# A hybrid layer on one core: a table of steps for the inputs of the output projection, and token sums in pieces of two steps

## The chip, the cores and the metric

The kernel runs on one core of a Trainium2 chip. The metric is the device time of one execution in microseconds. The kernel before took 2541.38 us in the median of three runs (2538.63 to 2546.69). The profiled execution is another run, 2547.02 us long.

## The reference

One layer over 2176 tokens of width 1024: 128 context tokens and 2048 latent ones, in float32. For each token:

```python
h = rmsnorm(x, norm1) * (1 + scale1) + shift1
z = h @ w_in                                   # conv parts b, c, x; q, k, v, o, gates
y_sc = sc_b * conv3(sc_c * sc_x)               # short gated convolution, 512 wide
h_m  = rmsnorm(mlstm_bidir(q, k, v, gates)) * mh_norm * sigmoid(o)   # 4 heads of 128
x = x + gate1 * (concat([y_sc, h_m]) @ w_out)  # the output projection
h2 = rmsnorm(x, norm2) * (1 + scale2) + shift2
a, g = split(conv3(h2 @ w_up))                 # 2 x 2816 wide, conv over the grid
x = x + gate2 * ((silu(g) * a) @ w_down)
```

It returns the normalised x of both token groups and the final scan states of the context.

## The kernel before

Float32 products are made of three TensorE products each: every operand is split into a high part (a copy that rounds, on ScalarE) and a low part (the difference, on VectorE or GpSimd), and high*high, low*high and high*low are added up in PSUM (lines 221 to 223). A product of one 128-wide weight block with one block of up to 384 tokens is a *step* of 24 such matmuls. Tokens lie in six blocks: five of 384 and one of 256. The results of successive steps go to two PSUM buffers by turn (`acc`), so the product of step n+2 waits for the eviction of step n.

Names of tiles: `wst` is a weight as loaded (two buffers), `wh` and `wl` its split (four buffers); `xt` half a block of y as loaded (two buffers), `hH` and `hL` its split; `row` rows of results or of x; `F` a tile of 128x2304 with two buffers; `tH`, `tL` the split token sums. Tiles whose names end in D lie in DRAM. All DMAs are issued from one queue on SyncE (SP), which works in order: a DMA that must wait holds up those behind it.

The phases: modulation; v, gates, k, q and o products with scans of the gates; then three stretches that matter here.

1. **Sums weave.** Units of the backward chunk scan run beside the steps of the q and o heads. The o heads (`oD`) come last.
2. **Mix weave.** 34 units (17 chunks, two pairs of heads) of the mLSTM itself run beside 1.6 steps each. The steps are first the 36 of the short convolution (four output rows, three blocks, three products), then the output projection's 48: three groups of two token blocks, sixteen steps in a group (four pairs of output rows; in each pair two steps of the one block and two of the other). Each group needs y, which convolution and units have written to DRAM, loaded and split (L506, L517, L518). The evictions of the output projection are L604, its squares L566 and their sum L572; `stats` (five steps behind a group's end) makes the factors rc that the normalisation needs. In a unit, `queries` and `weigh` make R (L972, L976), which the y products (L986, L988) use; `denom` begins with the update of the forward state sf (L995), then come the denominators and in `heads` the division.
3. **Sums and up-projection.** The up-projection multiplies by sums of token blocks, seven forms ("slots" 0 to 6, used in the order 6, 0, 1, 5, 2, 4, 3), in the manner of Strassen. `sums` makes them in pieces beside the last steps of the output projection: a piece loads two stretches of x, scales them (L272, L274), forms four sums (L276 to L279), splits some of them straight into a slot (L283, L284: "direct") and stores the others (L287). A slot that isn't split directly is loaded again by `get_f` (L302) and split by `put_f` (L312, L313). The products of the up-projection are L1206 to L1208, from 1106.41 us on; the down-projection follows.

Until the Mix weave a scheduler orders the instructions; from the first Mix instruction on (`first`) every engine runs them in the order in which the program emits them (`in_order`).

Of the kernel before, what the change touches and what calls it, by code (L numbers as in the profile page):

```python
# [10 lines left out]
F32 = mybir.dt.float32  # L11
# [7 lines left out]
P = 128  # L19
# [38 lines left out]
def hymba_kernel(ctx: ExitStack, tc: tile.TileContext, I, O):  # L58
# [182 lines left out]
    def sums(hf, pool, qs=range(2), direct=()):  # L241

        for q in qs:
# [18 lines left out]
            nf = load(0)  # L262
            yield
            for kk in range(4):
                f = nf
                if kk < 3:
                    nf = load(kk + 1)
                for i, k in ((4, kk + 4), (6, kk)):
                    x = f[:, i * w:(i + 2) * w]
                    for i0, n, v in ((0, P, 0), (P, 2 * w - P, 1)) if ts[0] == 0 else ((0, 2 * w, 1),):  # L270
                        e = i0 + n
                        V.scalar_tensor_tensor(x[:, i0:e], x[:, i0:e], ab[:, 1, k, v:v + 1], rb[:, i0:e],  # L272
                                               op0=ALU.mult, op1=ALU.mult)
                        S.activation(x[:, i0:e], x[:, i0:e], AF.Identity, bias=modT[:, 24 + k, v:v + 1])  # L274
# [13 lines left out]
                if kk < 3:  # L288
                    yield
# [62 lines left out]
    with ExitStack() as ph1:  # L352
# [24 lines left out]
        def vg(blocks, hs, ws):  # L377
            for b in blocks:
                hH, hL = hs[b]
                for j in range(2):  # L380
                    for c in chunks(b):
# [8 lines left out]
                        r = rq.tile([P, 2, 129], F32, name="rv", bufs=4)  # L390
# [30 lines left out]
        def shortconv(blocks, hs, then=None, more=(), ws=None):  # L421
# [3 lines left out]
            ws = [] if ws is None else ws  # L425
            ws += [load_w(next(todo)) for _ in range(3)]
# [15 lines left out]
            for m in range(4):  # L442
                wc, wx, wb = ws[:3]
                del ws[:3]
                for j, b in enumerate(blocks):
                    t0, n = BL[b]
                    store()
                    if then and m == 3 and j:
                        then(j - 1, 0)
# [3 lines left out]
                    if j < 2:  # L453
                        get()
                    else:
                        split()
                    yield
                    acc = gemm(wx, hs[b], n)
# [13 lines left out]
                    if then and m == 3 and j:  # L472
                        then(j - 1, 1)
                    yield
                    acc = gemm(wb, hs[b], n)
# [6 lines left out]
                    if then and m == 3 and j:  # L482
                        then(j - 1, 2)
# [15 lines left out]
        def get_y(b):  # L499

            assert done >= set(chunks(b))
            t0, n = BL[b]
            yts = []
            for kh in range(2):
                yt = xp.tile([P, 4, 384], F32, name="xt")
                Q.dma_start(yt[:, :, :n], yD[4 * kh:4 * kh + 4, :, t0:t0 + n].rearrange("k p t -> p k t"))  # L506
                yts.append(yt)
            return yts

        def split_y(b, yts, kh):  # L510

            n = BL[b][1]
            if kh == 0:
                early[b] = h_pair()
            yH, yL = early[b]
            for k in range(4):
                S.activation(yH[:, 4 * kh + k, :n], yts[kh][:, k, :n], AF.Copy)  # L517
                V.tensor_sub(yL[:, 4 * kh + k, :n], yts[kh][:, k, :n], yH[:, 4 * kh + k, :n].bitcast(F32))  # L518

        held_y = {}  # L520

        def load_y(b, step):
            if step == 0:
                held_y[b] = get_y(b)
                if b:
                    next(outs)
            else:
                split_y(b, held_y[b], step - 1)

        def next_y(grp, ready):  # L530


            for b, may in zip(grp, ready):
                while not done >= set(chunks(b)):
                    yield
                yts = get_y(b)
                yield
                for kh in range(2):
                    while not may():
                        yield  # L540
                    split_y(b, yts, kh)
                    yield

        def out_proj(grps, defer, ws):


# [27 lines left out]
            rows, got, behind, squared, held, sss, past = [], [], [], [], [], {}, set()  # L574
            for k in range(2):
                load_r(k)
            ny = iter(())
            yield
            for k, (g, m, b) in enumerate(steps):
                grp, (t0, n) = grps[g], BL[b]  # L580
                if k % 16 == 0 and g + 1 < len(grps):
                    ny = next_y(grps[g + 1], (lambda: True, lambda b=grp[0]: (b, KT - 1) in past))
# [11 lines left out]
                if k % 16 >= 5:  # L594
                    next(ny, None)
# [10 lines left out]
                past.add((b, m))  # L606
                behind.append((b, m, xr))
                if k % 16 == 15:
                    run(ny)
                    held = [k, grp]  # L610
                if k == len(steps) - 1:
                    for x in squared + [close(*x) for x in behind]:
                        add(*x)
                    defer.append(lambda: stats(grp, [sss[b] for b in grp]))
                yield
# [315 lines left out]
        class Mix:  # L931
# [58 lines left out]
            def denom(self):  # L990
                c, hp, sf = self.c, self.hp, sfs[self.hp]
                if 0 <= c < NL - 1:
                    for h in range(2):
                        r = c * 4 + 2 * hp + h
                        V.scalar_tensor_tensor(sf[:, h], sf[:, h], decB[:, r:r + 1], self.sb[:, h, 0],  # L995
# [473 lines left out]
```

## Time and profile before

| | us |
|---|---|
| median of 3 runs (lowest to highest) | 2541.38 (2538.63 to 2546.69) |
| profiled execution | 2547.02 |
| its span, first to last instruction | 2545.2 |
| TensorE busy (share) | 2464.8 (97%) |
| VectorE busy (share) | 1664.6 (65%) |
| ScalarE busy (share) | 1122.8 (44%) |
| GpSimd busy (share) | 573.7 (23%) |
| mean granted TensorE clock | 0.987 |
| last head product done, first shortconv product | 621.5, 629.75 |
| first product of the up-projection | 1106.41 |

Engines are PE (TensorE), DVE (VectorE), ACT (ScalarE), POOL (GpSimd) and SP (SyncE, which issues the DMAs). A row of a timeline gives start and duration, the line of the kernel, the operation with its tiles, a count, and in brackets the idle time before it with what ended it. In the table of windows each engine's busy time and count is followed by the granted clock of TensorE, the DMA engines' busy share and GB/s.

### The profile page before, as it was taken

The numbers are of one execution on the slowest core, as the hardware profiler recorded it, in microseconds if no ns is written. First come the engines' busy times: TensorE is split into PE (matmuls) and PEld (weight loads), VectorE is DVE, ScalarE is ACT, GpSimd is POOL, SyncE is SP. The second block draws the span as 40 slices with busy tenths as digits, with TensorE's granted clock in tenths as the row PEclk, the third lists the DMA queues.
The fourth block names the chain that finished last, engine by engine and source line by source line (L and its number), as shares of the span: only waits on it lengthen the run. The fifth ranks groups of instructions, "written<-read, shape, count | busy, mean of one in ns | idle before, by whom it ended". The sixth has DMA issues, their size and how long they took to land.

```text
span 2545.2 us, 42525 instructions
## 1 busy us (share of the span) xinstructions
PE 2464.8 (97%) x16127; PEld 2360.4 (93%) x16127; DVE 1664.6 (65%) x2670; ACT 1122.8 (44%) x2059; POOL 573.7 (23%) x501
## 2 busy tenths in 40 slices
PE   7999999998999999889999999899999999999998
PEld 7999999998999989889999999788888899999998
DVE  3993552331556676688677666877767786787586
ACT  4421162333444554455444444555545554444342
POOL 2442242110343443322122111221221100000000
PEclk9999999999999999999999999999999999999999
DMA  8873873455666876755224122522222276867674
GB/s 282 279 241 116 305 242 96 126 177 166 209 208 204 285 243 221 250 199 174 83 99 165 73 74 83 183 98 84 92 98 84 80 248 207 251 195 225 188 222 133
DMA packets 281424, 444.60 MB, mean 175 GB/s; under 512 B 23283, under 2 KB 206723, under 8 KB 279555
## 3 DMA queue, kind: packets, MB, share of 16 engines
q1 hardware_dynamic: 281218, 441.88, 52.9%
q8 instruction: 127, 2.08, 0.3%
q14 instruction: 79, 0.64, 0.1%
HBM read 335.31 MB, written 106.48 MB: 174 GB/s over the span
## 4 chain that ended last, share of the span: by engine, by line
PE 68%; DVE 5%; DMA 4%; issue 2%; ACT 1%; POOL 0%; SPq 0%; DVEq 0%; ACTq 0%; POOLq 0%
PE pa L1206 7%; PE pa L1208 6%; PE pa L1207 6%; PE d L1361 5%; PE d L1362 5%; PE d L1360 5%; PE acc L221 4%; PE acc L223 4%; PE acc L222 4%; PE pb L1206 3%; PE pb L1207 3%; PE pb L1208 3%; PE pc L1206 2%; PE pc L1207 2%; PE pc L1208 2%
## 5 line engine op out<-in xcount | busy, mean ns | idle before, releaser
L221 PE MATMUL acc<-hH,wh 128*128 128x384 f32 (+1 forms) x1536 | 514.6, 335 | 23.3 <-DVE row L604 14.6
L223 PE MATMUL acc<-hH,wl 128*128 128x384 f32 (+1 forms) x1536 | 507.8, 331 | 0.4 <-POOL wl L130 0.4
L222 PE MATMUL acc<-hL,wh 128*128 128x384 f32 (+1 forms) x1536 | 506.7, 330 | 0.0
L1206 PE MATMUL pa<-tH,wh 128*128 128x288 f32 (+1 forms) x1056 | 348.7, 330 | 12.1 <-issue 7.3
L1360 PE MATMUL d<-bh,wh 128*128 128x272 f32 x1232 | 356.7, 290 | 0.7 <-ACT raw L1218 0.7
L1362 PE MATMUL d<-bh,wl 128*128 128x272 f32 x1232 | 357.1, 290 | 0.0
L1361 PE MATMUL d<-bl,wh 128*128 128x272 f32 x1232 | 356.3, 289 | 0.0
L1208 PE MATMUL pa<-tH,wl 128*128 128x288 f32 (+1 forms) x1056 | 347.9, 329 | 1.0 <-DVE wl L331 1.0
L1207 PE MATMUL pa<-tL,wh 128*128 128x288 f32 (+1 forms) x1056 | 347.6, 329 | 0.0
L331 POOL TENSOR_TENSOR wl<-st,wh 128x512 fp32r<-128x512 f32 x132 | 185.3, 1403 | 704.3 <-ACT wh L330 677.8
L130 POOL TENSOR_TENSOR wl<-wst,wh 128x512 fp32r<-128x512 f32 (+1 forms) x160 | 236.5, 1501 | 419.2 <-ACT wh L127 373.1
L221 PEld LDWEIGHTS acc<-hH,wh 128*128 128x128 f32 x1536 | 292.6, 190 | 26.2 <-issue 15.4
L222 PEld LDWEIGHTS acc<-hL,wh 128*128 128x128 f32 x1536 | 292.8, 191 | 0.3 <-issue 0.2
L223 PEld LDWEIGHTS acc<-hH,wl 128*128 128x128 f32 x1536 | 292.0, 190 | 1.1 <-POOL wl L130 0.9
L1149 DVE SCALAR_TENSOR_TENSOR tt<-raw,fw,tt 128x127 f32<-128x127 f32 (+4 forms) x264 | 246.4, 955 | 2.7 <-ACT tt L1155 1.4
L1360 PEld LDWEIGHTS d<-bh,wh 128*128 128x128 f32 x1232 | 232.9, 189 | 1.3 <-ACT raw L1218 1.1
L1361 PEld LDWEIGHTS d<-bl,wh 128*128 128x128 f32 x1232 | 232.9, 189 | 0.2
L1362 PEld LDWEIGHTS d<-bh,wl 128*128 128x128 f32 x1232 | 232.9, 189 | 0.0
L1206 PEld LDWEIGHTS pa<-tH,wh 128*128 128x128 f32 x1056 | 199.3, 189 | 28.8 <-issue 8.3
L1208 PEld LDWEIGHTS pa<-tH,wl 128*128 128x128 f32 x1056 | 199.9, 189 | 17.0 <-DVE wl L331 1.4
L1207 PEld LDWEIGHTS pa<-tL,wh 128*128 128x128 f32 x1056 | 199.5, 189 | 15.6
L330 ACT ACTIVATE wh<-s 128x512 fp32r<-128x512 f32 x176 | 110.9, 630 | 175.2 <-PE pc L1207 92.6
(248 smaller groups left out, 4849.8 us busy)
## 6 DMA issues: line engine op xcount, KB each, us to landing
st<-in_w_up SPq DMA_DIRECT2D x88, 512.0 KB, 3.9
us<-uD SPq DMA_DIRECT2D x48, 544.0 KB, 4.9
wst<-in_w_in SPq DMA_DIRECT2D x48, 512.0 KB, 4.9
uD<-tt SPq DMA_DIRECT2D x44, 544.0 KB, 2.7
R<-nD SPq DMA_DIRECT2D x34, 512.0 KB, 4.2
wm<-in_w_modr SPq DMA_DIRECT2D x32, 512.0 KB, 5.5
wst<-in_w_out SPq DMA_DIRECT2D x24, 512.0 KB, 6.9
st<-wsD SPq DMA_DIRECT2D x32, 384.0 KB, 3.5
```

Source lines behind the costliest of these rows:

```text
L130: G.tensor_sub(wl[:, a:a + n // 2], st[:, a:a + n // 2], wh[:, a:a + n // 2].bitcast(F32))
L221: PE.matmul(acc[:, :n], w_h, hH[:, k, :n], start=(k == 0), stop=False)
L222: PE.matmul(acc[:, :n], w_h, hL[:, k, :n], start=False, stop=False)
L223: PE.matmul(acc[:, :n], w_l, hH[:, k, :n], start=False, stop=(k == KT - 1))
L331: (G if on_pool else V).tensor_sub(wl, a, wh.bitcast(F32))
L1149: V.scalar_tensor_tensor(o, i, w, o, op0=ALU.mult, op1=ALU.add)
L1206: PE.matmul(acc, wh[:, w], rh, start=(kk == 0 and i in (0, 1, 5)), stop=False, skip_group_check=True)
L1207: PE.matmul(acc, wh[:, w], rl, start=False, stop=False, skip_group_check=True)
L1208: PE.matmul(acc, wl[:, w], rh, start=False, stop=(kk == 3), skip_group_check=True)
L1360: PE.matmul(acc, wh[:, c], uh, start=(kk == 0), stop=False)
L1361: PE.matmul(acc, wh[:, c], ul, start=False, stop=False)
L1362: PE.matmul(acc, wl[:, c], uh, start=False, stop=(kk == KH - 1))
```

## The change

1. The first three weights of the short convolution are loaded and split after ten of the twelve o-head steps, in the Sums weave (`first_w`, `ahead_w`), where before `shortconv` did it at its start.
2. The loads and splits of y are taken apart. A class `Feed` holds a table: for each block at which step, and whether ahead of its product or behind it, a load, four copies (`lead`) or two or three subtractions (`trail`) are emitted.
3. The update of the forward state is a stage of its own, `state`, behind `heads`.
4. A piece of the token sums takes two steps. In the first one product by rb over both stretches, with scale and bias on ScalarE; in the second the sums, direct splits and the store. Both first loads stand at the head. Slots 6 and 0 are both split directly in both halves, so half a slot's `get_f` and `put_f` fall away. `until` says at which steps the pieces run (59 to 71 and 73 to 81, counted from the first convolution step).
5. `stats` comes four steps behind a group's end instead of five; the tile `rv` of the v products is taken from the pool of `row`.

The number of matmuls is the same.

```diff
-            nf = load(0)
+            fs = [load(0), load(1)]
             yield
             for kk in range(4):
...
+                f = fs.pop(0)
+                x = f[:, 4 * w:8 * w].rearrange("p (a t) -> p a t", a=2)
+                V.tensor_tensor(x, x, bc(rb[:, None, :2 * w], [P, 2, 2 * w]), op=ALU.mult)
+                for i, k in enumerate((kk + 4, kk)):
+                    for a, e, v in spans(ts[0], ts[0] + 2 * w):
+                        a, e = a - ts[0], e - ts[0]
+                        S.activation(x[:, i, a:e], x[:, i, a:e], AF.Identity, bias=modT[:, 24 + k, v:v + 1],
+                                     scale=ab[:, 1, k, v:v + 1])
+                if kk in (1, 2):
+                    fs.append(load(kk + 1))
+                yield
...
-                yield
                 i0, i1 = int(0 in direct), 7 - int(6 in direct)
                 Q.dma_start(tDs[hf][i0:i1, :, c0:c1].rearrange("i p t -> p i t"), f[:, i0:i1])
-                if kk < 3:
-                    yield
+                yield
...
+        def first_w(blocks):
+            return [load_w(I["w_in"][o]) for o in (4, 8, 0)]
...
-        def split_y(b, yts, kh):
...
-            for k in range(4):
-                S.activation(yH[:, 4 * kh + k, :n], yts[kh][:, k, :n], AF.Copy)
-                V.tensor_sub(yL[:, 4 * kh + k, :n], yts[kh][:, k, :n], yH[:, 4 * kh + k, :n].bitcast(F32))
...
+        class Feed:
+            def __init__(self, grps):
+                self.step, self.plan, self.yt = 0, {}, {}
+                for g, (a, b) in enumerate(grps):
+                    for b_, at in ((a, ((-8, 0, self.load, 1), (-6, 0, self.load, 0), (-6, 1, self.lead, 1),
...
+                                   (b, ((-3, 0, self.load, 1), (-2, 1, self.load, 0), (-2, 1, self.lead, 1),
+                                        (-1, 0, self.trail, (4, 5, 6)), (-1, 1, self.lead, 0),
+                                        (0, 0, self.trail, (7, 0, 1)), (1, 0, self.trail, (2, 3))))):
+                        for k, late, f, arg in at:
+                            self.plan.setdefault((36 + 16 * g + k, late), []).append((f, b_, arg))
+            def __call__(self, late=False):
+                for f, b, arg in self.plan.get((self.step, int(late)), ()):
+                    f(b, arg)
+                self.step += late
...
-                if held and k == held[0] + 5:
+                if held and k == held[0] + 4:
...
+        def ahead_w():
+            wo.extend(first_w(BA))
+            return
+            yield
+
+        fill = chain(heads(BA, hs, 12, qD, AF.Copy, QS), islice(og, 10), ahead_w(), og)
...
-               (-3, "third"), (-1, "heads"), (-2, "scale"), (1, "exps")))
+               (-3, "third"), (-1, "heads"), (-1, "state"), (-2, "scale"), (1, "exps")))
...
-        slots = {6: slot(6, "right")}
-        side = sums(0, fpool, (0,), (6,))
-        for _ in fill:
-            next(side, None)
+        slots = {i: slot(i, "right") for i in (6, 0)}
+        until(36, sums(0, fpool, (0,), (6, 0)))
+        run(islice(fill, 1))
...
-        for _ in chain(side, sums(0, fpool, (1,), (6, 0))):
-            run(islice(outs, 1))
-        f = get_f(0, 0, (0,))
-        run(islice(outs, 1))
-        put_f(f, 0, 0, (0,))
-        run(islice(outs, 1))
+        until(46, sums(0, fpool, (1,), (6, 0)))
```

How the order changes at three places. First, SP's queue at the end of the Sums weave, where the first shortconv weights are loaded. Before (`R`, `k`, `v`, `q` are inputs of scan and units):

```order
L884 DMA v_6374<-vD 128x258
L879 DMA q_6376<-qD 128x2x128
L950 DMA R<-nD 128x1024
L405 DMA oD<-row 128x384
L119 DMA wst<-in_w_in 128x1024 x4
L879 DMA k_6435<-kD 128x2x128
```

After, three of the four stand between 39 and 72 rows further ahead; the last of the three:

```order
L920 DMA sD<-sb 128x516
L404 DMA oD<-row 128x384
L876 DMA v_6010<-vD 128x258
L119 DMA wst<-in_w_in 128x1024
L404 DMA oD<-row 128x384
L920 DMA sD<-sb 128x516 x2
```

and at the old place:

```order
L871 DMA q_6397<-qD 128x2x128
L942 DMA R<-nD 128x1024
L404 DMA oD<-row 128x384
L119 DMA wst<-in_w_in 128x1024
L871 DMA k_6435<-kD 128x2x128
```

One weight, the fourth, is left behind the last store of the o heads.

Second, VectorE in the output projection, where the inputs of block 3 are split (`hL<-xt,hH`). Before:

```order
L572 TENSOR_TENSOR ss<-ss,sq 128x384
L518 TENSOR_TENSOR hL<-xt,hH 128x384 x4
L604 SCALAR_TENSOR_TENSOR row<-acc,modT,row 128x384
L972 TENSOR_TENSOR R<-R,q_9527 128x2x256
L995 SCALAR_TENSOR_TENSOR sf_4975<-sf_4975,decB,sb 128x129 x2
L999 TENSOR_TENSOR den<-y,cols 128x4
L1000 SCALAR_TENSOR_TENSOR den<-y,den 128x4
L1001 RECIPROCAL den<-den 128x4
L976 TENSOR_TENSOR R<-S,R 128x2x256
L1035 TENSOR_TENSOR o_9623<-st,o_9623 128x256
L1011 SCALAR_TENSOR_TENSOR hv<-y,den,hv 128x128 x2
```

After:

```order
L964 TENSOR_TENSOR R<-R,q_9609 128x2x256
L986 TENSOR_TENSOR den<-y,cols 128x4
L987 SCALAR_TENSOR_TENSOR den<-y,den 128x4
L988 RECIPROCAL den<-den 128x4
L968 TENSOR_TENSOR R<-S,R 128x2x256
L1030 TENSOR_TENSOR o_9756<-st,o_9756 128x256
L998 SCALAR_TENSOR_TENSOR hv<-y,den,hv 128x128 x2
L1008 SCALAR_TENSOR_TENSOR sf_4979<-sf_4979,decB,sb 128x129 x2
L540 TENSOR_TENSOR hL<-xt,hH 128x384 x3
L569 TENSOR_TENSOR ss<-ss,sq 128x384
L597 SCALAR_TENSOR_TENSOR row<-acc,modT,row 128x384
L540 TENSOR_TENSOR hL<-xt,hH 128x384 x2
```

The four subtractions ahead of an eviction have become three and two in neighbouring steps, and the state's update has gone from between the two R rows to the end of the unit's rows.

Third, SP's queue at the end of the output projection: the last pieces' stores, and the loads of the slots that are not split directly. Before:

```order
L287 DMA tD_72<-F 128x5x288
L302 DMA F<-tD_72 128x1152
L555 DMA row<-in_x 128x256
L560 DMA xD<-row 128x256
L560 DMA xD<-row 128x384 x2
L302 DMA F<-tD_72 128x2304
L560 DMA xD<-row 128x256
L302 DMA F<-tD_72 128x2304
L560 DMA xD<-row 128x256
L318 DMA st<-in_w_up 128x1024
L302 DMA F<-tD_72 128x2304 x3
```

After:

```order
L552 DMA row<-in_x 128x256
L557 DMA xD<-row 128x256
L287 DMA tD_72<-F 128x5x288
L557 DMA xD<-row 128x384 x2
L557 DMA xD<-row 128x256
L301 DMA F<-tD_72 128x2304
L557 DMA xD<-row 128x256
L301 DMA F<-tD_72 128x2304 x3
L1168 DMA eD<-raw_11402 128x128
L317 DMA st<-in_w_up 128x1024
L301 DMA F<-tD_72 128x2304
```

The load of half a slot (128x1152) is gone, the last store stands behind the last load of x, and the first four slot loads stand closer behind it.

More of the change, by code (lines that the diff above doesn't have):

```diff
@@ L389, in vg @@
                             PE.matmul(acc[:, :264], a_l, w_h, start=False, stop=(k == KT - 1))
-                        r = rq.tile([P, 2, 129], F32, name="rv", bufs=4)
+                        r = rp.tile([P, 384], F32, name="row")[:, :258].rearrange("p (h d) -> p h d", h=2)
                         G.memset(r[:, :, 128:129], 1.0)
@@ L419, in heads, with shortconv @@
                     yield
-        def shortconv(blocks, hs, then=None, more=(), ws=None):
+        def first_w(blocks):
+            return [load_w(I["w_in"][o]) for o in (4, 8, 0)]
+        def shortconv(blocks, hs, more=(), ws=None, hook=None):
             todo = chain((I["w_in"][o + m] for m in range(4) for o in (4, 8, 0)), more)
-            ws = [] if ws is None else ws
-            ws += [load_w(next(todo)) for _ in range(3)]
+            ws = first_w(blocks) if ws is None else ws
+            todo = islice(todo, 3, None)
+            hook = hook or (lambda late=False: None)
             got, stores = [], []
@@ L447, in shortconv @@
                     store()
-                    if then and m == 3 and j:
-                        then(j - 1, 0)
+                    hook()
                     acc = gemm(wc, hs[b], n)
@@ L471, in shortconv @@
                         split()
-                    if then and m == 3 and j:
-                        then(j - 1, 1)
+                    hook(True)
                     yield
+                    hook()
                     acc = gemm(wb, hs[b], n)
@@ L481, in shortconv @@
                         get()
-                    if then and m == 3 and j:
-                        then(j - 1, 2)
+                    hook(True)
                     yield
@@ L520, in hymba_kernel @@
[L520 to L542, printed above, removed]
@@ L572, in add @@
                     V.tensor_add(sss[b][:, :n], sss[b][:, :n], sq[:, :n])
-            rows, got, behind, squared, held, sss, past = [], [], [], [], [], {}, set()
+            rows, got, behind, squared, held, sss = [], [], [], [], [], {}
             for k in range(2):
                 load_r(k)
-            ny = iter(())
             yield
@@ L580, in out_proj @@
                 grp, (t0, n) = grps[g], BL[b]
-                if k % 16 == 0 and g + 1 < len(grps):
-                    ny = next_y(grps[g + 1], (lambda: True, lambda b=grp[0]: (b, KT - 1) in past))
+                hook()
                 load_r(k + 2)
@@ L990, in denom @@
             def denom(self):
[L991 to L995, printed above, removed]
-                                               op0=ALU.mult, op1=ALU.add)
+                c, hp = self.c, self.hp
                 yv = self.yv = self.y[:, :, :258].rearrange("p h (d n) -> p h d n", d=2)
@@ L1014, in heads, with state @@
                     S.activation(sj, hv[:, h], AF.Square, scale=QS, accum_out=ss[:, h:h + 1])
+            def state(self):
+                c, hp, sf = self.c, self.hp, sfs[self.hp]
+                if 0 <= c < NL - 1:
+                    for h in range(2):
+                        r = c * 4 + 2 * hp + h
+                        V.scalar_tensor_tensor(sf[:, h], sf[:, h], decB[:, r:r + 1], self.sb[:, h, 0],
+                                               op0=ALU.mult, op1=ALU.add)
             def norm(self):
@@ L1081, in hymba_kernel @@
         wo = []
-        outs = out_proj(((0, 1), (2, 3), (4, 5)), late, wo)
-        fill = chain(heads(BA, hs, 12, qD, AF.Copy, QS), heads(BA, hs, 20, oD, AF.Sigmoid, 1.0))
+        grps = ((0, 1), (2, 3), (4, 5))
+        feed = Feed(grps)
+        outs = out_proj(grps, late, wo, feed)
+        feed.plan.setdefault((33, 0), []).append((lambda *_: next(outs), None, None))
+        og = heads(BA, hs, 20, oD, AF.Sigmoid, 1.0)
+        def ahead_w():
[3 more added lines that the diff above has]
+        fill = chain(heads(BA, hs, 12, qD, AF.Copy, QS), islice(og, 10), ahead_w(), og)
         with tc.tile_pool(name="ms", bufs=1, side="right") as ms:
@@ L1087, in hymba_kernel @@
         run(fill)
-        fill = chain(shortconv(BA, hs, load_y, [I["w_out"][m] for m in range(2)], wo), islice(outs, 37))
+        fill = chain(shortconv(BA, hs, [I["w_out"][m] for m in range(2)], wo, feed), outs)
         mb = phr.enter_context(tc.tile_pool(name="mb", bufs=1, side="right"))
```

56 lines of the change are left out of this document (27 added, 29 removed).

## The prediction

> **What bounds the kernel now.** I read the head of the page first, then TensorE's waits in the stretch that the change touches (600 to 1200 us), then the windows table, and last the timelines of the engines around the largest waits; from those single rows are picked (start, duration, line, operation, count, and in brackets the idle time before it and what ended it).
>
> ```profile
> span 2545.2 us, 42525 instructions
> ...
> PE 2464.8 (97%) x16127; PEld 2360.4 (93%) x16127; DVE 1664.6 (65%) x2670; ACT 1122.8 (44%) x2059; POOL 573.7 (23%) x501
> ```
>
> TensorE is busy 97% and its matmuls stay the same, so only its idle time, and time at a slow clock, can be won. The waits (in total, times, longest):
>
> ```profile
> PE acc L221 <- DVE row L604: 14.6, 6, 3.9
> PE acc L221 <- ACT wh L127: 8.2, 1, 8.2
> PE pa L1206 <- issue: 7.3, 1, 7.3
> PE y L988 <- DVE R L976: 3.5, 3, 1.3
> PE y L986 <- DVE R L972: 2.8, 1, 2.8
> ...
> PE acc L223 <- POOL wl L130: 0.4, 1, 0.4
> ```
>
> These 36.8 us are nearly all of it. A wait also costs afterwards, as the column of the granted clock (PEclk, after POOL's) shows in windows behind the waits, and in two long ones:
>
> ```profile
> 700.00:800.00 100.00, 100.00 (x657) 100.00 (x656) 56.14 (x135) 48.83 (x152) 42.34 (x46) 1.00 0.66 205
> 820.00:960.00 140.00, 129.75 (x822) 128.66 (x822) 98.87 (x213) 73.39 (x228) 57.84 (x58) 0.96 0.79 257
> 629.70:636.50 6.80, 6.35 (x19) 5.84 (x20) 0.00 (x0) 1.84 (x2) 4.99 (x4) 0.50 0.32 96
> 898.20:902.50 4.30, 4.30 (x16) 4.30 (x17) 4.23 (x11) 1.18 (x5) 1.60 (x1) 0.63 0.87 259
> 1066.00:1070.30 4.30, 4.22 (x15) 4.25 (x16) 4.30 (x4) 1.82 (x3) 3.71 (x3) 0.60 1.03 370
> 1083.80:1088.00 4.20, 4.15 (x24) 4.18 (x25) 4.20 (x4) 1.79 (x3) 3.70 (x3) 1.00 0.71 236
> 1106.40:1111.70 5.30, 5.29 (x25) 5.30 (x26) 5.27 (x8) 4.10 (x7) 0.00 (x0) 0.57 0.81 294
> ```
>
> The quiet weave (700 to 800) does 6.57 matmuls a us. The stretch 820 to 960, where the inputs of the output projection are split, does 822 in 140 us; at the quiet rate 920. The missing 98 are 98/6.57 = 14.9 us. A slow spell costs length times (1 - clock): 3.4 us after the first weights, 1.6 at 898, 1.7 at 1066, 2.3 at 1106, none at 1083.8.
>
> **First weights.** The end of the head products, and the first shortconv weight:
>
> ```profile
> 623.14 0.95 SPq L119 DMA_DIRECT2D wst<-in_w_in  x2
> 628.64 1.06 ACT L127 ACTIVATE wh<-wst 128x1024 fp32r<-128x1024 f32 x1 [1.51 <-DMA wst<-in_w_in]
> 629.83 4.99 POOL L130 TENSOR_TENSOR wl<-wst,wh 128x512 fp32r<-128x512 f32 x4 [4.01 <-ACT wh L127]
> 629.75 0.69 PE L221 MATMUL acc<-hH,wh 128*128 128x384 f32 x1 [8.23 <-ACT wh L127]
> wst<-in_w_in SPq DMA_DIRECT2D x48, 512.0 KB, 4.9
> ```
>
> The loads stand in SP's queue behind the last oD store and are issued at 623.14, after the last head product (629.75 - 8.23 = 621.5). In the change the three stand some 40 to 70 queue entries further ahead, among the Sums units' loads, and 4.9 of transfer, 1.06 of copy and 2.5 of subtraction a weight (half of 4.99) are done long before 621.5, on ACT and POOL, beside TensorE (before 629.83 POOL was idle for 4.01, waiting for wh). Removed: 8.2 of wait, 0.4 for wl, 3.4 of slow clock: **12.0**. The load that is left at the old place, the fourth weight, is wanted nine steps later. Against it: two staging buffers serve the three loads, so the third waits on SP until the first is split, and k and v loads wait behind it. If that holds up the Sums units by one copy and one subtraction (3.5), 8.5 is left; I take 12.0.
>
> **The state update** (L995, two instructions) leaves the way between scores and the second y product:
>
> ```profile
> 675.07 3.12 POOL L130 TENSOR_TENSOR wl<-wst,wh 128x512 fp32r<-128x512 f32 x2 [2.55 <-ACT wh L127]
> 676.97 2.68 DVE L995 SCALAR_TENSOR_TENSOR sf<-sf,decB,sb 128x129 f32<-128x129 f32 x2
> 680.78 0.49 PE L988 MATMUL y<-v,R 128*128 128x129 f32 x2 [1.30 <-DVE R L976]
> ```
>
> That wait and a twin of 1.05 at 819 are 2.4 us; without up to 2.68 ahead of it R is in time. I take **2.0**, since other DVE work may fill the place; between 0 and 2.4. The update's next reader is a whole unit later, so nothing waits for it there.
>
> **The feed of the output projection.** Before, four copies and four subtractions run as one lump, in front of the eviction that TensorE waits for:
>
> ```profile
> 892.23 2.87 POOL L130 TENSOR_TENSOR wl<-wst,wh 128x512 fp32r<-128x512 f32 x2 [6.81 <-ACT wh L127]
> 888.34 0.55 DVE L572 TENSOR_TENSOR ss<-ss,sq 128x384 f32<-128x384 f32 x1
> 892.60 4.92 DVE L518 TENSOR_TENSOR hL<-xt,hH 128x384 fp32r<-128x384 f32 x4 [3.71 <-ACT hH L517]
> 897.45 0.60 DVE L604 SCALAR_TENSOR_TENSOR row<-acc,modT,row 128x384 f32<-128x384 f32 x1
> 898.20 0.42 PE L221 MATMUL acc<-hH,wh 128*128 128x384 f32 x1 [2.66 <-DVE row L604]
> 949.49 0.42 PE L221 MATMUL acc<-hH,wh 128*128 128x384 f32 x1 [3.68 <-DVE row L604]
> 1027.89 0.41 PE L221 MATMUL acc<-hH,wh 128*128 128x384 f32 x1 [3.86 <-DVE row L604]
> ```
>
> The lump takes 4.92 beside POOL's subtractions, 1.2 each, where one of that shape and operation takes 0.55. The table puts two or three in a step: 1.7 at 0.55 each, 3.7 at 1.2, in steps of 4.3 to 6.5 us whose eviction is needed only a step later (acc has two buffers). So no single step should hold TensorE as long. At stake: 14.9, and the same lump for the last block, 3.86 plus 1.6 of slow clock: 20.4 together. The work itself stays, seven of the sixteen subtractions of a group still fall into steps that have POOL's weight subtractions, and the second block of each group is tight:
>
> ```profile
> xt<-yD SPq DMA_DIRECT2D x10, 768.0 KB, 6.4
> ```
>
> its second load is issued one step, 4.3 to 6.5 us, before its copies, and takes 6.4; the copies then hold ACT, and the subtractions behind them DVE, for up to 2.1 us, with R, evictions and squares queued behind. I leave one wait for each of the three groups, 1.2 (the mean of the three R waits, 3.5/3) and a slow spell of 1.6: 8.4. Gain **12.0**. Bounds: 20.4 if nothing is left, 3.9 if each group keeps one wait of 3.9 and 1.6.
>
> The Trainium skill speaks against so much (page "SBUF — State Buffer", section "SBUF: two separate sides"): a VectorE operation with two SBUF inputs and a GpSimd one that reads SBUF share a port pair as an exclusive lock, held for the whole instruction. The 1.2 beside POOL against 0.55 agrees; by that rule the delay goes with the overlap and not with the lumping, and with 7/16 of it left the term would be 11.5 instead of 12.0.
>
> **The sums' pieces** run beside steps 59 to 81. Of the six L604 waits, the three above are 10.2; the other 4.4 are here, with 1.7 of slow clock (1066): 6.1. A piece still takes two steps; one product by rb replaces two or three, some of the scaling goes to ACT, and direct splits of slot 0 are added (0.45 on DVE, 0.45 on ACT in each piece of the first half). About as much DVE work stands between the evictions, differently cut. I leave two waits of 1.2 and one slow spell of 1.7: gain **2.0**, between -2 (that cut worse by as much) and 6.1. rv in the row pool adds no instruction on TensorE and lies in a part where DVE and ACT are half idle: 0.
>
> **The start of the up-projection.** Not a product but a chain of the token sums sets it:
>
> ```profile
> 1095.76 0.32 SPq L302 DMA_DIRECT2D F<-tD  x1
> 1110.61 10.52 SPq L302 DMA_DIRECT2D F<-tD  x3
> 1099.11 1.16 ACT L312 ACTIVATE tH<-F 128x1152 fp32r<-128x1152 f32 x1 [6.10 <-DMA F<-tD]
> 1126.52 2.23 ACT L312 ACTIVATE tH<-F 128x1152 fp32r<-128x1152 f32 x2 [0.22 <-DMA F<-tD]
> 1100.30 1.36 DVE L313 TENSOR_TENSOR tL<-F,tH 128x1152 fp32r<-128x1152 f32 x1 [6.36 <-ACT tH L312]
> 1105.83 0.48 DVE L604 SCALAR_TENSOR_TENSOR row<-acc,modT,row 128x256 f32<-128x256 f32 x1
> 1106.41 0.58 PE L1206 MATMUL pa<-tH,wh 128*128 128x288 f32 x1 [7.29 <-issue]
> ```
>
> The "issue" wait of 7.29 is the last evictions standing behind L313, which waited for slot 0's half. That half goes, and with it this wait; but the first column of products also needs five slots through two F buffers, issued from 1095.76 on and copied by 1128.75, 33.0 us later. After the change the store of the last piece stands about one step (4.3) later, and the chain is about 4.7 shorter without the half. What TensorE doesn't wait at the first product it waits inside the column: **+1.0**. Bounds: -4.3 (the later store alone) and 9.6 (7.3 and the 2.3 of slow clock, the chain not deciding).
>
> **Sum:** 12.0 + 2.0 + 12.0 + 2.0 + 1.0 = 29.0. The profiled execution took 2547.0 us, 5.6 above the median of the runs, 2541.4; so 2518.0 for its like, and **2512** for the median.
>
> **Rivals.**
> - Only the first weights' gain holds; DVE's work and POOL's overlap are what they were, so that the waits move to other steps. For it: DVE is busy 98.87 of the 140 us from 820 to 960. Against: 30% is free. 2541.4 - 12.0 = 2529.
> - All waits go but the slot chain: 12.0 + 2.4 + 20.4 + 6.1 + 1.0 = 41.9, 2499. Against: the tight second load.
> - A short wait leaves the clock alone. Then the three spells of 1.6 and the one of 1.7 that I kept fall away: 6.5 more, 2506. For it: 1.00 after the 1.87 at 1083.8. Against: 0.63 after 2.66 at 898, 0.60 after 1.86 at 1066. The Trainium skill has it so (page "TensorE: Matmul & The Clock Gate", "What's actually happening"): half clock only after an idle window of about 3.4 us; the two spells here came after shorter waits, so the measurement decides.
> - The change doesn't do what it says: the first weights' copies stay behind the last head evictions, and the table's copies wait for xt as the lumps did. Left are 2.0 + 2.0 + 1.0: 2536, no change.
> - Slower: SP's queue. A piece's load waits in it for the store of the piece two before (two F buffers), and y and weight loads wait behind. If six pieces come late by 5 us each, with 1.7 of slow clock, 40 us are lost against 29 won: 2552. It decides from 3.1 us late (6 x (3.1 + 1.7) = 29). Against: the kernel before has the same two buffers and its waits there sum to 4.4.
>
> **How the numbers follow.** Forecast 0.57 (own range 2503 to 2522), only the first weights 0.18, all waits gone 0.10, clock left alone 0.06, not as it says 0.05, slower 0.04. Range 2497 to 2532: from all waits gone with some of the slot chain, to the first weights alone with part of the start's -4.3. A measurement here tells about 0.3%, 7.6 us, from no change: faster 0.91, same 0.05, slower 0.04.
>
> **What would show it.** No wait for wh at the first shortconv product, clock 1.00 behind it; 6.57 matmuls a us nearly kept in the steps that split y; no L604 wait over 2 us; a wait of several us inside the first column of the up-projection in place of the "issue" wait. A wait for F from xD of over 3 us, or of k and v loads behind a weight in the Sums units, would make it wrong.

## The result and the profile after

The changed kernel takes 2513.74 us in the median of four runs (2512.76 to 2518.03); the kernel before, beside it, 2541.32. The ratio is 0.9892, 95% interval 0.9872 to 0.9912: 27.6 us faster, where 29.0 were forecast.

The head of the page of the changed kernel:

```profile
span 2511.2 us, 42476 instructions
...
PE 2456.8 (98%) x16127; PEld 2352.3 (94%) x16127; DVE 1636.5 (65%) x2649; ACT 1123.3 (45%) x2062; POOL 577.5 (23%) x501
```

The spans differ by 34.0, more than the medians, since the profiled execution of before was 5.6 above its median. TensorE's waits of the changed kernel between 600 and 1200 us:

```profile
PE acc L221 <- DVE row L597: 4.1, 2, 2.7
PE pa L1212 <- ACT sq L563: 3.9, 1, 3.9
PE pc L1214 <- POOL wl L330: 2.5, 1, 2.5
PE acc L223 <- POOL wl L130: 2.3, 3, 0.8
PE acc L221 <- ACT wh L127: 1.5, 2, 1.2
PE st L252 <- ACT rb L254: 1.0, 2, 0.5
PE pb L1214 <- DVE wl L330: 1.2, 1, 1.2
PE pa L1212 <- ACT wh L329: 0.8, 1, 0.8
PE pa L1212 <- ACT tH L311: 0.7, 1, 0.7
```

They sum to 18.0 where the same list of the kernel before sums to 40.4. The wait of 8.2 for wh, the waits for R and four of the six for evictions are gone; new are those for weights in the up-projection (L1212, L1214). Windows of the changed kernel: the head products' end and the start of the convolution, the stretch of the Mix weave in which y is split, and three spells behind a wait:

```profile
620.30:629.00 8.70, 8.70 (x52) 8.67 (x51) 0.00 (x0) 3.50 (x5) 1.23 (x1) 1.00 0.78 250
800.00:940.00 140.00, 140.00 (x927) 140.00 (x926) 92.26 (x227) 78.07 (x236) 67.16 (x63) 1.00 0.84 276
983.80:988.00 4.20, 4.17 (x24) 4.20 (x25) 3.85 (x7) 3.02 (x7) 0.75 (x1) 1.00 0.92 302
1005.40:1009.00 3.60, 3.50 (x12) 3.53 (x13) 3.35 (x7) 2.35 (x5) 0.08 (x1) 0.53 0.66 220
1071.20:1077.00 5.80, 5.79 (x24) 5.80 (x25) 3.03 (x6) 1.46 (x3) 0.00 (x0) 0.50 0.97 333
```

The second row answers to the 822 matmuls of before: 927 in 140 us, 6.62 a us, TensorE busy throughout at full clock. No idle time is left to win there. DVE's busy time went from 98.87 to 92.26 only.

Where the time went can be read from the starts of TensorE's steps in both traces. The table gives, stretch by stretch, how much shorter the profiled execution was than that of before, from the first of the 24 head products of the Sums weave on; a minus sign means longer. A product of the up-projection is counted as twelve matmuls, so 28 products are two columns.

| stretch | changed | changed, again | late weights | state first | old places | old places, step's head | both undone | before, one move |
|---|---|---|---|---|---|---|---|---|
| to the first convolution step | 8.5 | 8.5 | 1.1 | 8.5 | 8.5 | 8.5 | 8.5 | 0.5 |
| 36 convolution steps | 12.5 | 12.5 | 10.0 | 10.9 | 8.0 | 9.5 | 4.7 | -0.2 |
| output projection, steps 0 to 22 | 10.4 | 10.4 | 10.4 | 10.4 | 5.3 | 10.4 | 0.6 | 9.8 |
| output projection, the rest | 3.9 | 3.9 | 3.9 | 3.8 | 5.4 | 4.8 | 4.9 | 3.3 |
| to the first product of the up-projection | 3.4 | 3.4 | 3.4 | 3.5 | 3.4 | 3.4 | 3.4 | 1.4 |
| its first 28 products | -10.2 | -8.6 | -10.1 | -9.8 | -10.3 | -8.6 | -9.0 | -0.4 |

The columns behind the first belong to the experiments. From there to product 60 the kernels of the table win back 0.3 to 1.1 us. What lies ahead of the first row varies by several us between executions of one kernel: the changed kernel reaches the first of these head products at 485.7 us, run again at 480.8. Of the 12.5 in the convolution, 3.6 stand in its first step (the slow clock behind the first weights), 1.6 and 1.3 behind two waits for R, and 5.9 in its last step, where the kernel before waited 2.80 for R with the clock at 0.67 behind it.

### The profile page after: what moved, and what is told of

It reads as the page before. It is cut to its first block, busy times and chain, and to the rows that moved or that the text cites. A ratio compares the mean times of both kernels' runs of the same rounds, so it can differ in the third digit from the quotient of the medians.

```text
span 2511.2 us, 42476 instructions
## 1 busy us (share of the span) xinstructions
PE 2456.8 (98%) x16127; PEld 2352.3 (94%) x16127; DVE 1636.5 (65%) x2649; ACT 1123.3 (45%) x2062; POOL 577.5 (23%) x501
## 4 chain that ended last, share of the span: by engine, by line
PE 81%; DVE 8%; DMA 5%; issue 2%; ACT 2%; POOL 1%; SPq 0%; DVEq 0%; ACTq 0%; POOLq 0%
PE acc L221 8%; PE acc L223 8%; PE acc L222 8%; PE pa L1212 6%; PE pa L1214 6%; PE pa L1213 6%; PE d L1367 5%; PE d L1368 5%; PE d L1366 5%; PE pb L1212 3%; PE pb L1214 3%; PE pb L1213 3%; PE pc L1212 2%; PE pc L1214 2%; PE pc L1213 2%
## 5 line engine op out<-in xcount | busy, mean ns | idle before, releaser
L1212 PE MATMUL pa<-tH,wh 128*128 128x288 f32 (+1 forms) x1056 | 350.0, 331 | 9.5 <-ACT sq L563 3.9
L1214 PE MATMUL pa<-tH,wl 128*128 128x288 f32 (+1 forms) x1056 | 348.1, 330 | 1.0 <-DVE wl L330 1.0
L1212 PEld LDWEIGHTS pa<-tH,wh 128*128 128x128 f32 x1056 | 199.9, 189 | 27.2 <-ACT sq L563 4.1
L1214 PEld LDWEIGHTS pa<-tH,wl 128*128 128x128 f32 x1056 | 200.8, 190 | 17.0 <-DVE wl L330 1.4
```

The costliest lines, as they stand in the source:

```text
L1212: PE.matmul(acc, wh[:, w], rh, start=(kk == 0 and i in (0, 1, 5)), stop=False, skip_group_check=True)
L1214: PE.matmul(acc, wl[:, w], rh, start=False, stop=(kk == 3), skip_group_check=True)
```

## The experiments

All were timed beside the kernel before on the same chip. In us, with the ratio to before:

| run | median | before | ratio (95%) |
|---|---|---|---|
| late weights | 2523.53 | 2540.38 | 0.9937 (0.9923 to 0.9950) |
| lumps beside GpSimd | 2520.94 | 2540.38 | 0.9923 (0.9910 to 0.9935) |
| lumps off GpSimd | 2519.50 | 2540.38 | 0.9917 (0.9904 to 0.9931) |
| state first | 2510.16 | 2540.38 | 0.9884 (0.9871 to 0.9898) |
| changed, again | 2511.50 | 2537.83 | 0.9890 (0.9876 to 0.9905) |
| old places | 2523.50 | 2537.83 | 0.9942 (0.9929 to 0.9954) |
| old places, step's head | 2512.54 | 2537.83 | 0.9901 (0.9888 to 0.9915) |
| old sums in the up-projection | 2507.20 | 2537.83 | 0.9881 (0.9866 to 0.9896) |
| both undone | 2527.10 | 2539.97 | 0.9952 (0.9939 to 0.9965) |
| last steps first | 2514.11 | 2539.97 | 0.9900 (0.9884 to 0.9916) |
| last steps first and old sums | 2504.98 | 2539.97 | 0.9863 (0.9847 to 0.9879) |
| before, lump at the step's head | 2528.19 | 2539.97 | 0.9954 (0.9939 to 0.9969) |

The ratio of the unaltered change, 0.9890 when run again and 0.9892 at first, is what the altered ones are measured against; 0.001 is 2.5 us.

> The changed kernel unaltered, as the measure for the three kernels beside it: the ratio to the kernel before as in its first runs, 0.989, within 0.002.

It came out as expected.

### The first weights

```diff
-        fill = chain(heads(BA, hs, 12, qD, AF.Copy, QS), islice(og, 10), ahead_w(), og)
+        fill = chain(heads(BA, hs, 12, qD, AF.Copy, QS), og)
...
-            ws = first_w(blocks) if ws is None else ws
+            ws = [] if ws is None else ws
+            ws += first_w(blocks)
```

> The changed kernel, with the first three weights loaded at the start of the short convolution again. My theory (the wait for wh, the missing wl and the slow clock behind it are worth 12.0 us, and nothing downstream absorbs them): 12 us slower than the changed kernel, 2514 + 12 = 2526, with one wait of about 8 for wh and the clock at 0.5 for 6 to 7 us behind it, and every later step as in the changed kernel. Rival (the later part, the start of the up-projection, absorbs an earlier or later arrival): under 6 us slower, 2520 or less.

Measured: 0.9937, so 0.0045 to 0.0047 or 11 to 12 us slower than the change. In the list of its waits one, of 7.4, is back:

```profile
PE acc L221 <- ACT wh L127: 9.0, 3, 7.4
```

In the table the first two rows lose 7.4 and 2.5 us, 9.9 together; all later rows are as in the changed kernel. So the wait was worth what it showed, and what was won there came through to the end. That one edit gives some four tenths of the gain.

### The split of y: four lumps instead of the table

Two tables put four copies and four subtractions in one place again, the first at steps in which GpSimd subtracts a weight, the second at the others:

```diff
-                    for b_, at in ((a, ((-8, 0, self.load, 1), (-6, 0, self.load, 0), (-6, 1, self.lead, 1),
-                                        (-5, 0, self.trail, (4, 5)), (-4, 0, self.trail, (6, 7)), (-4, 1, self.lead, 0),
...
+                    for b_, at in ((a, ((-8, 0, self.load, 1), (-6, 0, self.load, 0),
+                                        (-6, 0, self.lead, 1), (-6, 0, self.trail, (4, 5, 6, 7)),
+                                        (-5, 0, self.lead, 0), (-5, 0, self.trail, (0, 1, 2, 3)))),
+                                   (b, ((-3, 0, self.load, 1), (-3, 0, self.load, 0),
+                                        (-2, 0, self.lead, 1), (-2, 0, self.trail, (4, 5, 6, 7)),
+                                        (-1, 0, self.lead, 0), (-1, 0, self.trail, (0, 1, 2, 3))))):
```

In the second the lumps stand at -4 and -3 for a, at 0 and 1 for b, and b's loads at -3 and -2.

> The changed kernel with the table of steps altered: each half block is split in one lump of four copies and four subtractions, at steps in which GpSimd subtracts weights. Theory A (lumps ahead of an eviction are what TensorE waited for): the waits come back, 15 to 20 us slower than the changed kernel, 2529 to 2534. Theory B (the overlap with GpSimd, which makes a subtraction 1.2 instead of 0.55 us, is what costs): the same, since both are there. Rival C (neither; something else of the change removed the waits): under 3 us slower, 2517 or less.

> The same lumps of four, but at steps in which GpSimd subtracts no weights (steps 0 and 1 of four). Theory A (lumps): as slow as the lumps beside GpSimd, 10 us or more slower than the changed kernel, 2524 or more. Theory B (overlap): within 3 us of the changed kernel, 2511 to 2517, a lump taking 2.2 to 3.1 us instead of 4.9, no wait for L597 over 1 us in the weave.

Measured: 0.9923 and 0.9917, 6 to 8 us slower than the change, both. Neither theory held as it was put: lumps cost something at either place, but not the 15 to 20 us. The groups of y's subtractions on DVE between 780 and 1000 us (busy time, mean ns; idle before) in the kernel before, the changed one, the lumps beside GpSimd and the lumps off it:

```profile
L518 DVE TENSOR_TENSOR hL<-xt,hH 128x384 fp32r<-128x384 f32 x40 | 37.2, 990 | 14.7 <-ACT hH L517 14.7
```

```profile
L540 DVE TENSOR_TENSOR hL<-xt,hH 128x384 fp32r<-128x384 f32 x40 | 24.2, 652 | 3.1 <-ACT hH L534 3.1
```

```profile
L536 DVE TENSOR_TENSOR hL<-xt,hH 128x384 fp32r<-128x384 f32 x40 | 28.6, 776 | 18.9 <-ACT hH L530 18.8
```

```profile
L536 DVE TENSOR_TENSOR hL<-xt,hH 128x384 fp32r<-128x384 f32 x40 | 20.2, 565 | 19.1 <-ACT hH L530 19.1
```

Off GpSimd only two of the 40 subtractions are slowed, to 0.85 us (mean 565 ns; 550 undisturbed), and yet that kernel is no faster than the other. There the lump of a group's second block stands at steps 0 and 1, close to its product at step 2, and the list of its waits has the product itself waiting for a copy:

```profile
PE acc L221 <- ACT hH L530: 3.4, 1, 3.4
```

Counted as in the table, the lumps beside GpSimd lose 1.4 us in the convolution, 2.5 in steps 0 to 22 of the output projection and 4.8 in the rest of it, the lumps off it 1.6, 2.2 and 4.2. So the second run doesn't separate the overlap from lateness as meant. What both showed is that most of the weave's gain stays with lumps, when the loads come earlier than before and the lump stands at the head of its step. That asked for the old places.

### The old places, and the place inside a step

Both runs load and split at the steps of the kernel before: in the first group loads at -6 and -3 and lumps right behind them, in the others a's loads at -11 with lumps at -10 and -9, b's at -8 with lumps at -2 and -1. One difference is left: in the convolution the kernel before emits a lump at the end of its step, behind the eviction, and both runs emit it at the head of the same step. The first also emits the lump behind the weight's copy, just ahead of the product, by the edit below; the second leaves it at the head of the step.

```diff
-                hook()
                 load_r(k + 2)
...
                 w, xr = ws[m % 2], rows.pop(0)
+                hook()
                 acc = gemm(w, early[b], n)
```

> The changed kernel with loads and lumps of four at the very places of the kernel before: both loads one step ahead of the lumps in the first group, lumps at steps 6, 7, 14 and 15 of the other groups, and inside a step behind the weight's copy. The lumps beside GpSimd and the lumps off GpSimd each cost only some 6 to 8 us of the 20.4 that I had put down to the lumps. Theory D (place and lateness: a lump hurts when its load came only a step before, or when it stands behind the weight's copy, so that the eviction comes late): 15 to 20 us slower than the changed kernel, with waits for L598 of 2.5 to 3.9 as before. Rival (other parts, above all factors one step sooner and the state's update, had removed the waits): no more than with the other lumps, 6 to 9 us.

> The same steps, but inside a step at its head, ahead of the weight's copy and of GpSimd's subtractions. If the place inside the step is what matters: as the first lumps, 6 to 9 us slower than the changed kernel. If the step and the lateness of the load matter: as with the old places entirely, 15 to 20 us.

Measured, beside the change at 0.9890: 0.9942 behind the copy, 12 to 13 us slower, which lies between what theory and rival named; 0.9901 at the head, 1 to 3 us slower, not told from it, and less than was expected for either. In the table, steps 0 to 22 of the output projection lose 5.1 us in the one and nothing in the other: there the place inside the step decides, not which step it is and not the lumping. The convolution steps, where the two place the lump alike, lose 3.0 (head) and 4.5 us: in both the last step waits 1.85 or 1.86 for R, and only in the execution that lost 4.5 did the clock fall behind it (0.71 over 4.3 us, against 1.00). The rest of the difference in time lies in rows that the edit doesn't touch; the intervals leave room for it. The old places behind the copy in three engines' rows (ACT, POOL, DVE):

```profile
928.92 1.05 ACT L127 ACTIVATE wh<-wst 128x1024 fp32r<-128x1024 f32 x1
929.86 1.76 ACT L532 ACTIVATE hH<-xt 128x384 fp32r<-128x384 f32 x4
```

```profile
930.04 2.86 POOL L130 TENSOR_TENSOR wl<-wst,wh 128x512 fp32r<-128x512 f32 x2 [6.29 <-ACT wh L127]
```

```profile
930.41 4.92 DVE L538 TENSOR_TENSOR hL<-xt,hH 128x384 fp32r<-128x384 f32 x4 [3.19 <-ACT hH L532]
935.26 0.60 DVE L595 SCALAR_TENSOR_TENSOR row<-acc,modT,row 128x384 f32<-128x384 f32 x1
```

ScalarE copies the weight, which starts GpSimd's subtractions, and right behind it y's halves, which start DVE's. So the two always begin together: 1.2 us for each subtraction, and the eviction behind them 4.9 us late after DVE had idled for 3.19. The unaltered kernel before shows the same at 891 to 897; the rows of GpSimd and VectorE stand in the prediction, those of ScalarE are:

```profile
891.11 1.05 ACT L127 ACTIVATE wh<-wst 128x1024 fp32r<-128x1024 f32 x1
892.06 1.76 ACT L517 ACTIVATE hH<-xt 128x384 fp32r<-128x384 f32 x4
```

### The kernel before with that one move

```diff
+                if k % 16 >= 5:
+                    next(ny, None)
                 load_r(k + 2)
...
                 w, xr = ws[m % 2], rows.pop(0)
-                if k % 16 >= 5:
-                    next(ny, None)
                 acc = gemm(w, early[b], n)
```

> The kernel before with a single edit: in the output projection the lump of y (load or four copies and four subtractions) is emitted at the head of its step, ahead of the weight's copy and split, instead of behind them. Theory (the place inside the step is the cause of the waits behind lumps in the output projection): the waits at 898 and 949 go, 6 to 9 us faster than the kernel before, 0.997. Rival (they need the spreading as well): under 3 us.

Measured: 0.9954 (0.9939 to 0.9969), 12 us faster than before, with two lines moved: more than the 6 to 9 expected, and the waits at 898 and 949 are gone. In the table 9.8 of it stand in steps 0 to 22 of the output projection, where the whole change wins 10.4. The same lump now, ACT, POOL, DVE:

```profile
892.27 1.75 ACT L517 ACTIVATE hH<-xt 128x384 fp32r<-128x384 f32 x4
893.93 0.51 ACT L566 ACTIVATE sq<-row 128x384 f32<-128x384 f32 x1
894.34 1.04 ACT L127 ACTIVATE wh<-wst 128x1024 fp32r<-128x1024 f32 x1
```

```profile
895.46 2.99 POOL L130 TENSOR_TENSOR wl<-wst,wh 128x512 fp32r<-128x512 f32 x2 [6.69 <-ACT wh L127]
```

```profile
892.82 1.97 DVE L518 TENSOR_TENSOR hL<-xt,hH 128x384 fp32r<-128x384 f32 x4 [2.81 <-ACT hH L517]
894.70 0.55 DVE L572 TENSOR_TENSOR ss<-ss,sq 128x384 f32<-128x384 f32 x1
895.17 0.61 DVE L604 SCALAR_TENSOR_TENSOR row<-acc,modT,row 128x384 f32<-128x384 f32 x1
```

The lump is over in 1.97 us before GpSimd begins; over the stretch from 780 to 1000 us the mean of a subtraction fell from 990 to 689 ns. The waits for R in the convolution steps stay, as they must (this edit doesn't touch those): the row of the table for the convolution is unchanged.

### The state's update, alone and together with the old places

```diff
-               (-1, "out"), (0, "scores"), (-3, "turn"), (0, "queries"), (-2, "norm"), (-1, "denom"), (0, "weigh"),
-               (-3, "third"), (-1, "heads"), (-1, "state"), (-2, "scale"), (1, "exps")))
+               (-1, "out"), (0, "scores"), (-3, "turn"), (0, "queries"), (-2, "norm"), (-1, "state"), (-1, "denom"), (0, "weigh"),
+               (-3, "third"), (-1, "heads"), (-2, "scale"), (1, "exps")))
```

> The changed kernel with the update of the forward state ahead of the denominators again, between the making of the two R. My theory: waits for R (the second y product on L968) of 1.0 to 1.3 us come back where GpSimd subtracts weights beside it, 2 to 2.5 us in all, 2516. Rival (the y feed alone had removed them, since the update is late only behind a lump): 0 to 0.5 us, 2514.

> The changed kernel with both undone: the y feed at its old places behind the weight's copy, and the state's update ahead of the denominators. The old places alone made it 12 us slower; the weave as a whole had gained 18.9 us without the first weights. Theory (the two add up: 12 and 1.6): 2525, the rest of the weave's gain from something else. Rival (they multiply, since the update beside GpSimd stands behind a lump and pushes the next one): 2530 or more, the weave's length (first convolution step to the first sums) within 2 us of the kernel before, less its 3.9 us of slow start.

Alone, the trace loses 1.6 us in the convolution steps, with one wait for R of 1.3 back. The time, 0.9884 against 0.9890 and 0.9892, can't show so little. With the old places as well the time is 0.9952, 16 us slower than the change; the table loses 7.8 and 9.8 us in the convolution steps and the first 23 of the output projection, against 4.5 and 5.1 from the old places alone. The two don't add: 17.6 together, 9.6 and 1.6 apart. Its waits:

```profile
PE acc L221 <- DVE row L595: 10.3, 3, 4.2
...
PE y L976 <- DVE R L962: 3.1, 1, 3.1
PE y L978 <- DVE R L966: 2.4, 2, 1.3
```

With both undone the weave has only 5.3 us less than before, of which 3.6 are the slow start behind the first weights (3.9 in the expectation). The time that my second theory named, 2530 or more, wasn't reached, but its test on the weave's length was met (1.7 us from before). So the table of steps and the update's place are, together, all of the weave's gain but 1.7 us; how the update's 0.6 to 2.7 us and a late lump push each other from one unit to the next I did not follow further.

### The start of the up-projection

```diff
-        side = sums(1, fpool)
+        side = sums1(1, fpool)
```

Here `sums1` is the function `sums` of the kernel before.

> The changed kernel with the old pieces (two products on VectorE, eight steps) for the second half's token sums, which run beside the up-projection. The changed kernel lost 7.4 us between the start of the up-projection and its second column against the kernel before, 5.2 of it as waits for wl and wh between 1112 and 1120 us. Theory (the new pieces' work on ScalarE and VectorE delays the splits of the second column's weights): these waits go, 4 to 6 us faster than the changed kernel. Rival (the weights come late from SP's queue, which now issues them behind the slot loads): the waits stay, within 1 us.

The loss of 7.4 us named there was read too low: by the starts of the matmuls it is 10.2, as in the table.

In the changed kernel two of the waits of the second column, and ScalarE ahead of the later one:

```profile
1112.53 0.41 PE L1214 MATMUL pb<-tH,wl 128*128 128x288 f32 x1 [1.16 <-DVE wl L330]
1120.13 0.41 PE L1214 MATMUL pc<-tH,wl 128*128 128x288 f32 x1 [2.55 <-POOL wl L330]
```

```profile
1111.32 0.81 ACT L271 ACTIVATE F<-F,modT,ab 128x512 f32<-128x512 f32 x1
1113.29 1.28 ACT L1175 ACT_TABLE_LOAD   x1 [1.16 <-DVE tt L1155]
1114.58 1.12 ACT L1175 ACTIVATE tt<-tt 128x1088 f32<-128x1088 f32 x1
1115.60 0.61 ACT L329 ACTIVATE wh<-s 128x512 fp32r<-128x512 f32 x1
```

The weight's copy stands behind the pieces' scaling and a table load that waited for DVE. With the old pieces these waits are gone, and products 16 to 28, nearly all of the second column, take as long as before, where the change had lost 6.5 to 6.8: 4.5 of waits, and most of the rest a slow clock (0.68 over the 3.6 us behind the wait of 2.55). About 1.7 us of that come back later. The time, 0.9881 against 0.9890, is in that direction but not clear by itself.

```diff
-        ahead = [next(prods) for _ in range(2)]
         run(fill)
+        ahead = [next(prods) for _ in range(2)]
```

> The changed kernel with the last two steps of the output projection emitted ahead of the first two weights of the up-projection instead of behind them. Theory (the wait of 3.9 before the first product of the up-projection is for PSUM, held by the last evictions, and these stand on VectorE behind the weights' subtractions, 1.4 us, and a wait of 0.7 for their copies): that wait falls to about 2, and 1.5 to 2.5 us are won in all, since the slot loads too stand behind the last rows' stores. Rival (the store of the last piece and the slot loads behind it set the first column): nothing is won in all, within 0.7 us, the wait going into the column.

> Both edits that looked like a gain in the up-projection: last two steps first, and the old pieces for the second half's sums. If they add: 4 to 6 us faster than the changed kernel, ratio to the kernel before 0.987. If the first column takes up what the earlier start gives: as the old sums alone, 0.988.

With the last two steps first the wait of 3.9 before the first product leaves the list, and the up-projection starts 1.2 us sooner behind the last step; a wait of 1.3 for the squares' sum of the last block appears (L496) and that for the weights grows to 3.1. The time is 0.9900: nothing is won. With both edits it is 0.9863 (0.9847 to 0.9879), 2504.98 us, about 7 us under the change by the ratios and the lowest time of the study; the intervals of the two still overlap by 0.0003 to 0.0007, so that it is faster than the change is likely, not shown.

No run undoes the new pieces beside the output projection, or the earlier `stats`. Their share is known from the rows of the table alone.

## Why the prediction was right, and where its parts were not

The time was inside the range and 2 us from the forecast. So close a hit is luck: two terms missed in opposite directions. The gain of the weave was put about 8 us too low, that of the start of the up-projection 6 to 8 us too high.

- **First weights**, 12.0: against the kernel before 8.5 in the first row and 3.6 in the first step, 12.1; undone alone, 9.9 in the trace and 11 to 12 in the time. Right. That the third load holds up SP did not show as a wait in the list.
- **State's update**, 2.0: 1.6 in the trace alone, more together with lumps.
- **Feed**, 12.0. Without the first weights' slow clock the weave (convolution steps and 23 of the output projection) won 12.5 + 10.4 - 3.6 = 19.3, where my terms for it were 2.0 and, for two groups, 14.9 - 5.6 = 9.3. The step that failed is "I leave one wait for each of the three groups": two did not come; the third did, at 1005.50, 2.74 long and with the clock at 0.53 behind it:

```profile
983.83 0.41 PE L221 MATMUL acc<-hH,wh 128*128 128x384 f32 x1 [1.36 <-DVE row L597]
1005.50 0.66 PE L221 MATMUL acc<-hH,wh 128*128 128x384 f32 x1 [2.74 <-DVE row L597]
```

  The reason I gave was not the right one either. I wrote that lumping was the fault and that spreading would mend it. The runs show that the lump's place behind the weight's copy was, for the output projection: moved ahead of it, the old lump costs the 12 us no longer. In the convolution nearly all of the feed's share is the one wait for R in the last step. The old steps bring 1.85 of it back, the update's old place alone none of it, and both together 3.1, as much as before (2.8). No run moves the place inside the step alone there, so what it does in the convolution stays open.
- **The port rule.** The Trainium skill (page "SBUF — State Buffer", section "SBUF: two separate sides") says that a GpSimd operation which reads SBUF and a VectorE operation with two SBUF inputs exclude each other for a whole instruction. The traces agree: a mean of 565 ns where the two hardly met, 990 where they met most. What I drew from it, that the gain goes with the overlap left over (7 of 16), did not hold as put: less was left, by the means (652 - 550) / (990 - 550) or about a quarter, and with next to no overlap the lumps still cost 6 to 7 us. What stands behind the slowed instructions at that moment, and whether the input is ready in time, counts as well.
- **Pieces of the sums**, 2.0 and the last block's share of the feed, 2.7: together 4.7, measured 3.9. Right in sum.
- **Start of the up-projection**, +1.0: measured 3.4 - 10.2 = -6.8 and, run again, 3.4 - 8.6 = -5.2. Wrong in sign and below the bounds (-4.3 to 9.6); the term's own two figures, 4.3 later and 4.7 shorter, would have given 0.4. Two things were missed. The first product still waits 3.9 us, since the last evictions now stand behind the first weights' work on DVE (with the last two steps emitted first, that wait is gone):

```profile
1071.21 0.58 PE L1212 MATMUL pa<-tH,wh 128*128 128x288 f32 x1 [3.92 <-ACT sq L563]
```

  and the new pieces are also used for the second half's sums, beside the up-projection, which I did not cost at all: 4.5 us of waits in the second column, 6.5 to 6.8 with the slow clock, and all of it gone with the old pieces.
- **Clock.** I kept a slow spell behind every wait. Behind 1.36 us the clock stayed at 1.00 (983.8), behind 2.74 and 3.92 it fell to 0.53 and 0.50; before, 1.86 had brought 0.60 once and 1.87 none. So a wait of 1.2, which I priced with a slow spell of 1.6, may well cost none. But the 3.4 us of idling that the page "TensorE: Matmul & The Clock Gate" of the Trainium skill names, in "What's actually happening", aren't needed.

Of the signs named, no wait for wh, the clock at 1.00 and 6.6 matmuls a us came. One wait for an eviction over 2 us was left (2.74), and the wait of several us stood ahead of the first product and in the second column, not in the first.

Of the rivals, "all waits go but the slot chain" came nearest to what happened in the weave; it was held off by the start of the up-projection.

## What to carry to other kernels

Look at what an in-order engine is made to start together. An instruction that releases work on GpSimd, put just ahead of one that releases work on VectorE, made the two collide again and again here (17 of the 40 subtractions between 780 and 1000 us were slowed, 5 after the swap). Swapping their places gave 12 us with two lines, and in the output projection nearly as much (9.8 against 10.4) as the table that spreads the work. And when a helper is rewritten for one stage, cost every other stage that calls it.

## What was not expected of the hardware

A subtraction of 128x384 on VectorE takes 0.55 us alone and 1.34 to 1.65 where GpSimd's subtractions hold it up in the kernel before. Over a stretch the mean went from 990 to 689 ns by the order of two instructions on a third engine, ScalarE, and to 565 at steps without GpSimd's. And a wait of TensorE of 1.86 us was once enough to bring the granted clock down to 0.60 for 4.3 us, while 1.87 was not another time. Even one and the same wait for R, in two kernels alike up to there, was followed by 0.71 in one execution (1.85 us) and by 1.00 in another (1.86 us). No run here tells what separates them.
